# Holding the transposes of the attention queries in the middle of the next product's first piece

## The chip, the cores and the metric

The kernel runs on one core of one Trainium2 chip. The metric is the device time of one execution in microseconds (us); lower is better. The engines are named as in the profile: PE is TensorE's matmul, PEld its weight load, DVE VectorE, ACT ScalarE, POOL GpSimd, SP SyncE.

## What is computed

The program is a decoder trunk of two layers over 256 tokens of 2048 features, all in float32. Layer 0 mixes tokens with a state-space model, layer 1 with attention; each is followed by a SwiGLU feed-forward block of width 5632, with RMSNorm ahead of every block and at the end. The change lies in the attention of layer 1:

```python
qkv = x @ w_qkv + b_qkv                      # 2048 -> 2048 (32 query heads of 64) + 2 x 256 (4 key/value heads)
s = einsum(q, k) * HEAD_DIM ** -0.5          # blocks of 128 queries against a window of two blocks of keys
s = s - slopes * dist                        # ALiBi; then keys outside the window of 128 are masked
m = maximum(max(s), sink)
p = exp(s - m)
p = p / (sum(p) + exp(sink - m))
o = einsum(p, v)
return o @ w_o
```

## The kernel before

**Products.** Every big product is cut into pieces. A piece takes 512 rows by 512 columns of a weight matrix. Weights and activations are kept as two parts each, a rounded high part and the rest, and a product adds three matmuls (L922, L923, L924: high by high, high by low, low by high). With four slices `a` of 128 rows and two halves `t` of 128 tokens, a piece is 4 x 2 x 3 = 24 matmuls of 128x128 by 128x512. `linear` (L937) runs the four pieces of a product with 2048 rows and leaves two accumulators in PSUM, one for each `t`.

**Weights.** `W.next()` at the head of each piece keeps the split of the weights three pieces ahead and their loads five: SP issues the load into `raw` (L109), ACT writes the high part (L122), DVE the low part (L127).

**Order.** The program is traced once and a scheduler lays out each engine's instructions: where an instruction's inputs are not ready by its estimate, it places a later one that is. What is placed on an engine then runs in that order. `tc.keep_in_program_order(ins)` pins one instruction behind the one traced just before it on the same engine; it adds order and no wait. Work that belongs between pieces is put into lists of functions: `left`, drained by `linear` after each piece, and `slots`, of which `linear` and the loop over O's pieces take one entry after each piece.

**Attention.** The keys and values come first, then the queries in four chunks `c` of 512 columns (eight heads). For a chunk, `linear` makes the accumulators; ACT scales the bias (L1309, pinned), and DVE writes the queries `act` from the accumulator, the norm's factor and the bias, one instruction for each `t` (L1312). `heads(c, q)` makes the functions for the rest:

- `turn_q`: eight PE transposes of `act` into two PSUM tiles `tr` (L1224), copied into `qT` by DVE for `t` = 0 and by ACT for `t` = 1 (L1225);
- `scores(g4)`: for four heads the score products (L1237, L1238), then on DVE the ALiBi bias and mask (L1241), the maximum (L1243 to L1246) and `es` (L1248), on ACT the exponentials with their sums (L1253), on DVE the sums (L1255), their reciprocal (L1256) and the scaling (L1258); for c < 3 the probabilities are turned by DVE in blocks (L1267) and through DRAM by DMAs of POOL (L985, L986);
- `turned_s`: for c = 3 the probabilities are transposed by PE (L1281);
- `values(g4)`: the products with the values (L1292 to L1296), cast by ACT (L1299) and split by DVE (L1300) into `oT`.

The slots that follow chunk `c` stand between the pieces of the next product, that is chunk `c + 1` or, for c = 3, the first two column blocks of the output projection O. After the first piece come `turn_q` and `scores(0)`, after the second the values of the chunk before and `scores(1)`, and so on.

In the state-space layer, `piece` (L926) is also called with a function `late`: it is called in the middle of the piece, after two of the four slices, and the first matmul of each later product of the piece is pinned. In the attention layer it is called without one.

Of the kernel before, what the change touches and what calls it, by code (L numbers as in the profile page):

```python
# [17 lines left out]
P = 128  # L18
# [38 lines left out]
def kernel(  # L57
# [6 lines left out]
    V, S, PL, PE = nc.vector, nc.scalar, nc.gpsimd, nc.tensor  # L64
    uid = [0]

    def nm(s):
        uid[0] += 1
        return f"{s}_{uid[0]}"
# [10 lines left out]
    def bank(shape, name="ps"):  # L80
        return ps.tile(shape, F32, tag="ps", name=nm(name))


    def turned_tile(name):
        return pp.tile([P, 2, 4, T], F32R, tag="b8", name=nm(name))
# [96 lines left out]
    ident = cp.tile([P, P], F32, name="ident")  # L182
# [6 lines left out]
    left = []  # L189

    slots = []


    def s5(early_piece):
# [725 lines left out]
    def products(acc, xq, w, a, t, first, last, keep=lambda ins: ins):  # L920
        x_ = xq[:, :, a, t * P : (t + 1) * P]
        keep(PE.matmul(acc, x_[:, 0], w[0][:, a], start=first, stop=False))  # L922
        PE.matmul(acc, x_[:, 0], w[1][:, a], start=False, stop=False)  # L923
        PE.matmul(acc, x_[:, 1], w[0][:, a], start=False, stop=last)  # L924

    def piece(acc, xq, first, last, late=None):  # L926

        w = W.next()
        for a in range(4):
            keep = lambda ins: ins  # L930
            if a == 2 and late:
                late()
                keep = tc.keep_in_program_order
            for t in range(2):
                products(acc[t], xq, w, a, t, first and a == 0, last and a == 3, keep)

    def linear(xt, n_pieces=None, halves=False):  # L937


        n_pieces = n_pieces or len(xt)  # L940
        acc = [bank([P, 512], "acc") for _ in range(2)]
        if halves:
            ws = [W.next() for _ in range(n_pieces)]
            for t in range(2):
                for q in range(n_pieces):
                    for a in range(4):
                        products(acc[t], xt[q], ws[q], a, t, q == 0 and a == 0, q == n_pieces - 1 and a == 3)
            return acc
        for q in range(n_pieces):
            piece(acc, xt[q], q == 0, q == n_pieces - 1)  # L950
            n = -(-len(left) // max(1, n_pieces - 1 - q))
            for _ in range(n):
                left.pop(0)()
            if slots:
                for f in slots.pop(0):
                    f()
        return acc
# [129 lines left out]
    def glu(norm):  # L1087
        def load_h(c):
            for t in range(2):
                cs = slice(512 * c, 512 * c + 512)  # L1090
                tc.keep_in_program_order(nc.sync.dma_start(h[:, c, t], x[t * P : (t + 1) * P, cs]))

        for c in range(NCH):
            left.append(partial(load_h, c))
            if c == 0:
                pa, pb = accs
                for _, half, q in G_ORDER[EARLY:8]:
                    piece(accs[half], gt[q], q == 0, q == 3)
                    if left:
                        left.pop(0)()  # L1100
            else:
                pa = linear(gt)
                pb = linear(gt)
            act = wp.tile([P, 2, 512], F32, tag="act", name=nm("act"), bufs=2)
            for t in range(2):
                hc = h[:, c, t]
                sg = act[:, t]
                S.activation(sg, pb[t], AF.Sigmoid)
                V.tensor_tensor(sg, pa[t], sg, op=ALU.mult)
                V.tensor_tensor(hc, hc, sg, op=ALU.add)  # L1110
                norm.chunk(c, t)

    def swiglu(norm, out_norm):
# [14 lines left out]
        def gu(c):  # L1128
            last = c == FF_GROUPS[-1][-1]
            pg = linear(norm.xt)  # L1130
            if r[0] is None:
                r[0] = norm.scale()
            sg = wp.tile([P, 2, 512], F32, tag="act", name=nm("act"), bufs=2)
            for t in range(2):
                S.activation(sg[:, t], pg[t], AF.Silu, scale=r[0][:, t : t + 1])
            pu = linear(norm.xt)
            for t in range(2):
                V.scalar_tensor_tensor(sg[:, t], pu[t], r[0][:, t : t + 1], sg[:, t], ALU.mult, ALU.mult)
            if last:
                left.append(lambda: turned(c, sg))  # L1140
                return
            o, v = turned_tile("hT"), block_tile()
            ht[c] = o
            left.extend(partial(blocks_turned, v, sg, tb) for tb in range(4))

            def split():
                S.activation(o[:, 0], v, AF.Copy)  # L1147
                V.tensor_tensor(o[:, 1], v, o[:, 0].bitcast(F32), op=ALU.subtract)

            left.append(split)  # L1150
# [21 lines left out]
    def attention(norm, out_norm):  # L1172
        with tc.tile_pool(name="at", bufs=1) as ap:
# [15 lines left out]
            def bias(c):  # L1189
                b = ap.tile([P, 512], F32, tag="bias", name=nm("bias"))  # L1190
                nc.sync.dma_start(b, b_qkv[0, 512 * c : 512 * c + 512].unsqueeze(0).to_broadcast([P, 512]))
                return b
# [3 lines left out]
            acc = linear(norm.xt)  # L1196
# [17 lines left out]
            ot = []  # L1214

            def heads(c, q):
                st = {}

                def turn_q():
                    st["qT"] = ap.tile([P, 4, 2, P], F32, tag="qT", name=nm("qT"), bufs=2)  # L1220
                    for t in range(2):
                        pt = bank([P, 4, P], "tr")
                        for a in range(4):
                            PE.transpose(pt[:, a], q[:, t, a * P : (a + 1) * P], ident)  # L1224
                        (S.copy if t else V.tensor_copy)(st["qT"][:, :, t], pt)  # L1225
                    ot.append(turned_tile("oT"))

# [57 lines left out]
                def values(g4):  # L1285

                    v0, v1 = (kv[:, t, 256 + HD * c : 256 + HD * c + HD] for t in range(2))
                    for i2 in range(2):
# [11 lines left out]
                        V.tensor_tensor(ot[c][:, 1, a], v, ot[c][:, 0, a].bitcast(F32), op=ALU.subtract)  # L1300

                return turn_q, scores, turned_s, values

            late = []

            for c in range(4):
                b = bias(c)
                acc = linear(norm.xt)
                tc.keep_in_program_order(S.mul(b, b, HD ** -0.5))  # L1309
                q = wp.tile([P, 2, 512], F32, tag="act", name=nm("act"), bufs=2)  # L1310
                for t in range(2):
                    V.scalar_tensor_tensor(q[:, t], acc[t], r8[:, t : t + 1], b, ALU.mult, ALU.add)  # L1312
                turn_q, scores, turned_s, values = heads(c, q)
                turned = [partial(turned_s, g4) for g4 in range(2)] if c == 3 else []
                late = late or [lambda: None] * 2
                slots.append([turn_q, partial(scores, 0)])
                slots.append([late[0], partial(scores, 1)])
                slots.append(turned[:1])
                late, mine = [partial(values, 0), partial(values, 1)], late
                slots.append([mine[1], *late[: len(turned) // 2]])  # L1320
            slots.extend([turned[1:], late[1:]])

            accs = [[bank([P, 512], "acc") for _ in range(2)] for _ in range(2)]
            for n, q in O_ORDER[:8]:
                piece(accs[n], ot[q], q == 0, q == 3)
                if slots:
                    for f in slots.pop(0):
                        f()
            for n in range(NCH):
                acc = accs[n] if n < 2 else linear(ot, 4)  # L1330
# [6 lines left out]
    accs = []  # L1337
# [15 lines left out]
    swiglu(n0, n1)  # L1353
    n2 = Norm(2, (0, 1, 2))
    attention(n1, n2)
    swiglu(n2, Last(None))

# [27 lines left out]
```

## Time and profile before

| what | value |
|---|---|
| median of 3 runs | 1981.99 us (1981.92 to 1982.06) |
| profiled execution | 1981.87 us |
| its span, first to last instruction | 1980.0 us |
| granted TensorE clock, mean | 0.993 |
| eight transposes of L1224, by c | begin at 1064.45, 1091.25, 1122.82 and 1155.35 us |
| queries of L1312 | 8 instructions, median 744 ns |

A row of the time line has the start, the time in us, the engine, the line, the operation, out<-in with partitions x elements, and a count where like rows are merged; a bracket gives the engine's idle time ahead of the row and what ended it. Rows of waits have the waiting engine and line, what it waited for, the sum in us, the number of times and the longest. A row of stretches has the stretch, its length, the busy time and count of each engine (PE, PEld, DVE, ACT, POOL), the granted clock, the DMA share and GB/s. All times count from the span's start.

### The profile page before, as it was taken

To read this page: it belongs to the slowest core of one execution; us is meant where nothing else is said; L and a number is where in the kernel's file an instruction comes from. 1 tells how busy PE (TensorE), PEld (TensorE's weight loads), DVE (VectorE), ACT (ScalarE), POOL (GpSimd) and SP (SyncE) were. 2 spreads that over 40 slices of the span, in tenths; PEclk is the share of its full clock that TensorE was granted. 3 is DMA by queue.
4 is the path that set the end of the run, shared out by engine and by line. 5 is a ranking of instruction groups with operands and counts; after the bars stand their busy time and mean duration, and the time that the engine had idled before them with its cause. 6 is when DMAs were issued, how large, how long until landed. Compare 5 with 4: busy or idle time off the path is not lost.

```text
span 1980.0 us, 24858 instructions
## 1 busy us (share of the span) xinstructions
PE 1936.3 (98%) x10336; PEld 1601.1 (81%) x10336; DVE 1271.8 (64%) x1652; ACT 859.1 (43%) x839; POOL 127.5 (6%) x117
## 2 busy tenths in 40 slices
PE   7699999999999999999999999999999999999998
PEld 6578888888888888888888778888888888888886
DVE  8956665666556646665577888666654665466545
ACT  6554444343334333433455554533333433333333
POOL 6840000000000000000010110000000000000000
PEclk9899999999999999999999999999999999999999
DMA  4036665556565565656575864666566556655664
GB/s 131 24 106 220 213 212 185 187 186 208 191 191 192 191 200 182 207 188 201 179 266 177 264 217 152 201 197 196 192 191 191 191 191 196 197 190 189 206 191 149
DMA packets 187845, 373.20 MB, mean 188 GB/s; under 512 B 11122, under 2 KB 11186, under 8 KB 187604
## 3 DMA queue, kind: packets, MB, share of 16 engines
q1 hardware_dynamic: 183168, 356.87, 56.0%
q0 software_dynamic: 3728, 12.60, 1.9%
q10 hardware_dynamic: 836, 2.14, 0.3%
q8 instruction: 81, 1.33, 0.3%
q14 instruction: 32, 0.26, 0.0%
HBM read 363.19 MB, written 8.39 MB: 188 GB/s over the span
## 4 chain that ended last, share of the span: by engine, by line
PE 91%; DVE 6%; ACT 1%; issue 1%; DMA 1%; POOL 0%; DVEq 0%; ACTq 0%
PE acc L922 29%; PE acc L923 29%; PE acc L924 29%; DVE scan L573 1%; DVE w L127 1%; DVE V L578 1%; DVE V L576 1%; PE pv L210 1%; PE py L798 0%; DVE sc L1258 0%; DMA pd<-bt 0%; PE px L210 0%; DVE mx L1243 0%; DVE bt L1267 0%; DMA raw<-in_attn_w_qkv_dram 0%
## 5 line engine op out<-in xcount | busy, mean ns | idle before, releaser
L127 DVE TENSOR_TENSOR w<-raw,w 128x2048 fp32r<-128x2048 f32 x330 | 757.0, 2294 | 591.2 <-ACT w L122 589.1
L122 ACT ACTIVATE w<-raw 128x2048 fp32r<-128x2048 f32 x332 | 636.2, 1916 | 842.0 <-PE acc L924 561.7
L922 PE MATMUL acc<-w,xT 128*128 128x512 f32 x1568 | 611.3, 390 | 0.0
L924 PE MATMUL acc<-w,xT 128*128 128x512 f32 x1568 | 610.4, 389 | 0.0
L923 PE MATMUL acc<-w,xT 128*128 128x512 f32 x1568 | 610.1, 389 | 0.0
L922 PEld LDWEIGHTS acc<-w,xT 128*128 128x128 f32 x1568 | 294.4, 188 | 62.5 <-issue 1.8
L924 PEld LDWEIGHTS acc<-w,xT 128*128 128x128 f32 x1568 | 294.3, 188 | 61.6 <-issue 0.3
L923 PEld LDWEIGHTS acc<-w,xT 128*128 128x128 f32 x1568 | 294.4, 188 | 60.6
L922 PE MATMUL acc<-w,hT 128*128 128x512 f32 x704 | 274.3, 390 | 0.0
L923 PE MATMUL acc<-w,hT 128*128 128x512 f32 x704 | 273.6, 389 | 0.0
L924 PE MATMUL acc<-w,hT 128*128 128x512 f32 x704 | 273.3, 389 | 0.0
L922 PEld LDWEIGHTS acc<-w,hT 128*128 128x128 f32 x704 | 132.1, 188 | 28.5 <-ACT hT L1124 1.2
L924 PEld LDWEIGHTS acc<-w,hT 128*128 128x128 f32 x704 | 132.2, 188 | 27.5
L923 PEld LDWEIGHTS acc<-w,hT 128*128 128x128 f32 x704 | 132.2, 188 | 27.2
L994 DVE STREAM_TRANSPOSE bt<-act 32x256 f32<-32x256 f32 x320 | 139.6, 436 | 5.5
L923 PE MATMUL acc<-w,gt 128*128 128x512 f32 x256 | 99.7, 390 | 0.6 <-DVE w L127 0.6
L922 PE MATMUL acc<-w,gt 128*128 128x512 f32 x256 | 99.8, 391 | 0.0
L924 PE MATMUL acc<-w,gt 128*128 128x512 f32 x256 | 99.6, 389 | 0.0
L985 POOL DMA_DIRECT2D pd<-bt x36 | 19.7, 553 | 945.8 <-DVE bt L1032 842.8
L1147 ACT ACTIVATE hT<-bt 128x1024 fp32r<-128x1024 f32 x20 | 21.2, 1061 | 106.6 <-DVE bt L994 106.6
L1159 DVE TENSOR_TENSOR h<-h,acc 128x512 f32<-128x512 f32 x64 | 42.9, 685 | 22.0 <-PE acc L924 22.0
L923 PEld LDWEIGHTS acc<-w,gt 128*128 128x128 f32 x256 | 48.1, 188 | 10.8 <-DVE w L127 1.0
(253 smaller groups left out, 1275.5 us busy)
## 6 DMA issues: line engine op xcount, KB each, us to landing
raw<-in_ffn_w_gate_dram SPq DMA_DIRECT2D x88, 1024.0 KB, 5.2
raw<-in_ffn_w_up_dram SPq DMA_DIRECT2D x88, 1024.0 KB, 5.2
raw<-in_ffn_w_down_dram SPq DMA_DIRECT2D x88, 1024.0 KB, 5.1
raw<-in_s_w_glu_dram SPq DMA_DIRECT2D x32, 1024.0 KB, 5.3
raw<-in_attn_w_qkv_dram SPq DMA_DIRECT2D x20, 1024.0 KB, 5.3
raw<-in_attn_w_o_dram SPq DMA_DIRECT2D x16, 1024.0 KB, 5.2
pd<-bt POOLq DMA_DIRECT2D x24, 192.0 KB, 3.8
pT<-pd POOLq DMA_DIRECT2D x6, 768.0 KB, 5.9
```

What stands on the lines that cost most here:

```text
L122: keep(S.activation(w[:, 0], self.raw[i], AF.Copy))
L127: keep(e.tensor_tensor(lo, self.raw[i], hi.bitcast(F32), op=ALU.subtract))
L210: return (lambda *a, **k: pin(f(*a, **k))) if self.on else f
L573: keep(V.tensor_tensor(t_, ws[..., part], bc(Vt[hf][:, k - 1, :, part], 1, 2), op=ALU.mult))
L576: V.tensor_tensor(v, v, t_[:, 0], op=ALU.add)
L578: V.tensor_tensor(v, v, t_[:, 1, ::-1], op=ALU.add)
L922: keep(PE.matmul(acc, x_[:, 0], w[0][:, a], start=first, stop=False))
L923: PE.matmul(acc, x_[:, 0], w[1][:, a], start=False, stop=False)
L924: PE.matmul(acc, x_[:, 1], w[0][:, a], start=False, stop=last)
L994: V.transpose(dst[32 * q : 32 * q + 32, :, :, 32 * tb : 32 * tb + 32], src[:, :, :, 32 * q : 32 * q + 32])
L1147: S.activation(o[:, 0], v, AF.Copy)
L1159: V.tensor_tensor(hc, hc, acc[t], op=ALU.add)
```

## The change

`turn_q` leaves the slot after the first piece and goes to a list `mids`. The first piece of the next product takes it from there and calls it as `late`: after the slices a = 0 and 1, twelve matmuls, and ahead of a = 2 and 3. The first of the eight transposes is pinned behind the matmuls traced ahead of it. The first matmul (L922) of each of the four remaining products of that piece is pinned too, as `piece` does with any `late`. `scores(0)` stays in the slot after the piece.

```diff
+    mids = []
...
         for q in range(n_pieces):
-            piece(acc, xt[q], q == 0, q == n_pieces - 1)
+            piece(acc, xt[q], q == 0, q == n_pieces - 1, mids.pop(0) if mids else None)
...
                         for a in range(4):
-                            PE.transpose(pt[:, a], q[:, t, a * P : (a + 1) * P], ident)
+                            ins = PE.transpose(pt[:, a], q[:, t, a * P : (a + 1) * P], ident)
+                            if t + a == 0:
+                                tc.keep_in_program_order(ins)
...
-                slots.append([turn_q, partial(scores, 0)])
+                mids.append(turn_q)
+                slots.append([partial(scores, 0)])
...
             for n, q in O_ORDER[:8]:
-                piece(accs[n], ot[q], q == 0, q == 3)
+                piece(accs[n], ot[q], q == 0, q == 3, mids.pop(0) if mids else None)
```

## The prediction

> **What bounds the kernel now.** I read the page's busy times first, then busy time by stretches, then who waited for whom inside the attention stretch, then PE's instructions one by one there. The page:
>
> ```profile
> PE 1936.3 (98%) x10336; PEld 1601.1 (81%) x10336; DVE 1271.8 (64%) x1652; ACT 859.1 (43%) x839; POOL 127.5 (6%) x117
> ```
>
> TensorE (PE) is busy 98% of the span. By stretches (us, then busy us of PE, PEld, DVE, ACT, POOL, then clock and DMA):
>
> ```profile
> 1060.00:1200.00 140.00, 136.32 (x822) 108.92 (x821) 115.10 (x160) 75.74 (x183) 17.65 (x30) 1.00 0.66 215
> 1200.00:1980.00 780.00, 771.15 (x3409) 638.13 (x3407) 480.06 (x465) 314.77 (x230) 0.00 (x0) 1.00 0.59 190
> ```
>
> The change acts only between 1060 and 1200. Behind it PE is busy for 771 of 780 us, so nothing there gives back time that the attention stage loses or gains: what PE gains or loses here moves the end one for one. What PE waited for in 1060 to 1200 (us in total, times, longest):
>
> ```profile
> PE tr L1224 <- DVE act L1312: 2.0, 2, 1.3
> PE at L1237 <- DVE qT L1225: 1.0, 1, 1.0
> PE acc L922 <- DVE oT L1300: 0.3, 1, 0.3
> ```
>
> So two waits belong to the change: the transposes (L1224) wait for the queries `act` from L1312, and the score products (L1237) wait for the copies `qT` (L1225). The change moves the transposes. The question is whether their input is ready at the new place.
>
> **Where the transposes stand now.** A piece is 24 matmuls of L922 to L924. For c=2 PE does this (start, duration, line):
>
> ```profile
> 1115.34 0.50 PE L922 MATMUL acc<-w,xT 128*128 128x512 f32 x1
> ...
> 1121.14 0.39 PE L923 MATMUL acc<-w,xT 128*128 128x512 f32 x1
> 1122.82 0.66 PE L1224 MATMUL tr<-ident,act 128*128 128x128 f32 x4 [1.29 <-DVE act L1312]
> 1123.23 0.48 PE L924 MATMUL acc<-w,xT 128*128 128x512 f32 x1
> 1123.54 0.60 PE L1224 MATMUL tr<-ident,act 128*128 128x128 f32 x4
> ```
>
> The first matmul of the next product starts at 1115.34, the 26th at 1121.14: 5.80 / 25 = 0.23 us each, the price of a matmul below. The transposes stand behind 26 of them (a 27th between their halves), not behind 24 as the code has them, and even so PE waits. After the change they stand behind 12, at 1115.34 + 12 x 0.23 = 1118.1. Their input comes from DVE:
>
> ```profile
> 1119.34 0.17 DVE L1255 TENSOR_TENSOR sm<-sm,es 128x8 f32<-128x8 f32 x1 [3.59 <-ACT sc L1253]
> ...
> 1122.02 1.40 DVE L1312 SCALAR_TENSOR_TENSOR act<-acc,r,bias 128x512 f32<-128x512 f32 x2
> ```
>
> L1312 could not have gone into DVE's idle 3.59 us, because it reads the scaled bias of L1309, which the code pins on ACT behind what was traced ahead of it:
>
> ```profile
> 1115.59 0.40 ACT L1253 ACTIVATE sc<-sc,mx 128x128 f32<-128x128 f32 x1 [5.20 <-DVE mx L1246]
> ...
> 1119.73 0.63 ACT L1309 ACTIVATE bias<-bias 128x512 f32<-128x512 f32 x1
> ```
>
> The exponentials of the heads before run from 1115.59, L1309 ends at 1120.36. So `act` for c=2 hangs on DVE and ACT, not on PE, and a transposing PE that comes four microseconds earlier waits four microseconds longer.
>
> **The change part by part.** No instruction is added or removed: per c, eight transposes and two copies are issued in another place; no DMA is, and no queue of SP or POOL is passed. The pins are order alone, on PE: the first transpose behind the first 12 matmuls, the later L922s behind the transposes. Unlike now, the scheduler can no longer fill a wait for `act` with matmuls of the same product: the other 12 of the piece and the scores stand behind the waiting transposes, and ACT's weight casts (L122), which wait for PE to free a weight buffer, behind those. Each c by itself:
>
> c=0. The queries (DVE) and the transposes (PE) stand here:
>
> ```profile
> 1058.59 1.41 DVE L1312 SCALAR_TENSOR_TENSOR act<-acc,r,bias 128x512 f32<-128x512 f32 x2 [0.59 <-PE acc L924]
> ```
>
> ```profile
> 1064.45 1.03 PE L1224 MATMUL tr<-ident,act 128*128 128x128 f32 x8
> ```
>
> Twelve matmuls earlier is 1064.45 - 2.76 = 1061.7, and `act` is whole at 1060.0: no wait. Now the scores follow the copies too closely (waits of the weight load at PE, 1064 to 1074):
>
> ```profile
> PEld at L1238 <- ACT qT L1225: 0.4, 1, 0.4
> PEld at L1237 <- DVE qT L1225: 0.4, 1, 0.4
> ```
>
> After the change 12 matmuls, 2.8 us, cover the copies. The two waits bound the gain between 0 and 0.8; some of it overlaps matmuls that drain, so I take -0.4.
>
> c=1. `act` comes from the first row (DVE), and PE's transposes now start at the second:
>
> ```profile
> 1088.30 1.40 DVE L1312 SCALAR_TENSOR_TENSOR act<-acc,r,bias 128x512 f32<-128x512 f32 x2
> ```
>
> ```profile
> 1091.25 1.04 PE L1224 MATMUL tr<-ident,act 128*128 128x128 f32 x8
> ```
>
> The new place is 1091.25 - 2.8 - 0.4 = 1088.1. The halves of `act` are ready at about 1089.0 and 1089.7: PE waits about 0.95 for the first and, with 0.4 of transposes between, 0.25 for the second. +1.2; 0 if DVE moves forward with c=0.
>
> c=2. PE arrives at 1118.1 + 0.8 = 1118.9 and waits until 1122.8: 3.9 us. What counts is the state behind it: when the second half of the transposes ends, just before 1124, PE has now done 27 matmuls of the product, and after the change 12. It is 15 x 0.23 = 3.45 us behind, which already contains c=0 and c=1, as the wait swallows both. Bounds: 0 if `act` came 3.9 earlier, 3.9 + 1.2 if DVE shifts with the 1.2 of c=1. I keep 3.45, since the rows of DVE and ACT above name no PE work as the last releaser.
>
> c=3. The next product is that of O, PE's rows:
>
> ```profile
> 1146.38 0.50 PE L922 MATMUL acc<-w,oT 128*128 128x512 f32 x1
> ...
> 1154.26 0.39 PE L923 MATMUL acc<-w,oT 128*128 128x512 f32 x1
> 1155.35 0.63 PE L1224 MATMUL tr<-ident,act 128*128 128x128 f32 x4 [0.70 <-DVE act L1312]
> ...
> 1160.38 0.50 PE L1237 MATMUL at<-kT,qT 64*128 64x128 f32 x4 [0.98 <-DVE qT L1225]
> ...
> 1161.99 0.44 PE L1292 MATMUL po<-pT,kv 128*64 128x128 f32 x4
> ...
> 1163.45 0.48 PE L1237 MATMUL at<-kT,qT 64*128 64x128 f32 x2
> ...
> 1166.39 0.50 PE L922 MATMUL acc<-w,oT 128*128 128x512 f32 x1
> ```
>
> From 1146.38 to 1154.26 start 35 matmuls, and a 36th stands between the halves. PE arrives at 1146.38 + 3.45 + 2.8 = 1152.6; if `act` comes when it does now, it waits 2.7 until 1155.35, and is then 36 - 12 = 24 matmuls, 5.5 us, behind. From here it wins: the transposes, the first scores and the second now stand close together, and PE waits at each. It waits 0.98 for the copy; the second scores take 1166.39 - 1163.45 = 2.94 where the first take 1161.99 - 1160.38 = 1.61, so 1.33 is lost; and 0.34 goes in the wait for oT. With 12 matmuls behind the transposes and a whole piece between the scores these 2.65 should fill up. 5.5 - 2.65 = +2.85. Bounds: +5.5 where the same chain of copies keeps PE waiting; about -0.2 where `act` of c=3 comes as PE does (3.45 - 0.7 - 0.3 - 2.65).
>
> Sum: +2.85 on the profiled execution's 1981.87 (1980.0 of span and 1.87 around it), or 1984.7; the median, 0.12 above that execution, gives 1984.8. Forecast 1984.8, own range 1982 to 1987.5.
>
> **The rivals.** First, the clock falls as well. Early in this trace PE stood idle for 4.19 us, and its clock in the stretches that follow was half (the number behind POOL's):
>
> ```profile
> 20.91 1.94 PE L210 MATMUL pu<-ident,xs 128*128 128x128 f32 x8 [4.19 <-DVE xs L210]
> ...
> 20.00:24.00 4.00, 3.02 (x13) 2.68 (x14) 3.90 (x9) 1.69 (x3) 4.00 (x5) 0.50 0.00 0
> 24.00:28.00 4.00, 4.00 (x74) 3.37 (x73) 3.90 (x7) 2.36 (x5) 4.00 (x5) 0.81 0.02 4
> ```
>
> Half speed lasted from 20.91 to about 24 + 4 x 0.19 / 0.5 = 25.5, 4.6 us, and cost 2.3. The waits of now, 1.29 and 0.70, left the clock of 1060 to 1200 at 1.00. The wait of 3.9 at c=2 is nearer to 4.19 than to 1.29, so once is possible: 1984.8 + 2.3 = 1987.1, twice 1989.4. Against it: 3.9 is a little less, and shrinks if DVE moves forward. The Trainium skill, "TensorE: Matmul & The Clock Gate", section "What's actually happening", speaks against the change in the same way: an idle window of about 3.4 us halves the clock, and the window runs freely. By that rule a wait of 3.9 holds a whole window only at some phases, and the sum would be 1984.8 or 1987.1 by the phase; the 4.19 us row agrees with it.
>
> Second, faster: L1309 comes ahead of the exponentials. The scheduler lays out ACT anew, and only L1309's pin behind the casts of the values (L1299) is fixed, not its place against L1253. If L1309 (0.63) goes ahead of the exponentials that begin at 1115.59, it ends at 1116.2, or one or two steps of its size later if the casts L1299 go first; DVE is idle then, and `act` of c=2 is whole 1.4 later, at 1117.6 to 1118.5, ahead of PE's 1118.9: no wait is left. At c=2 alone that decides little; at c=3 also, all waits of now go: 0.4 + 1.3 + 0.7 + 2.65 = 5.05, so 1977 to 1979. It is decided by whether `act` comes 3.9 us sooner than now; what is less leaves a part of the wait. Against it: the exponentials are traced ahead of L1309 and were placed ahead of it at c=2 with ACT idle for 5.20 before.
>
> Third, no change: `act` of c=3 comes with PE, the -0.2 above, or the gains of c=0 and c=3 pay for c=2: 1981 to 1982.5.
>
> **How the numbers follow.** Forecast 0.50, clock 0.20, no change 0.20, faster 0.10. A difference of 0.2%, 4 us, is about what a measurement of this kernel can tell: the bounds are 1978.0 and 1986.0. Slower by more: the clock's 0.20 and the upper part of the forecast (over +4 of a top of +5.5), 0.14: 0.34. Faster by more: 0.07 of the 0.10. Within: 0.59. The range leaves out the faster half of the faster case and the twice fallen clock: 1980 to 1989.
>
> **What would show it.** In the changed kernel's trace the eight transposes of each c stand behind 12 matmuls and not 24 to 36; PE waits for `act` L1312 at c=1, 2 and 3, in sum 7 to 8 us in place of 2.0; "PE at <- DVE qT" is gone; the second scores of c=3 take 1.6 us. The prediction is wrong if ACT's or DVE's order around L1309 and L1312 has changed, so that `act` is there when PE comes, or if other matmuls fill the wait, or if the copies again hold up the scores.

## Result and the profile after

The changed kernel takes 1995.16 us (median of 5 runs, 1992.88 to 1995.93) against 1981.92 us before on the same chip: the ratio is 1.006, with a 95% interval of 1.0049 to 1.0071. It is slower by 13 us. The forecast was 1984.8 us with a range up to 1989: the sign was right and the size far too small. The profiled execution has a span of 1993.1 us against 1980.0.

The page's line of busy times, then two stretches of the changed kernel (us, then busy us of PE, PEld, DVE, ACT, POOL, then the granted clock):

```profile
PE 1941.4 (97%) x10336; PEld 1605.9 (81%) x10336; DVE 1273.1 (64%) x1652; ACT 858.6 (43%) x839; POOL 127.5 (6%) x117
```

```profile
1060.00:1200.00 140.00, 127.48 (x743) 101.62 (x743) 109.56 (x154) 70.67 (x177) 17.64 (x30) 0.95 0.63 201
1220.00:1993.00 773.00, 764.20 (x3378) 632.70 (x3377) 474.66 (x458) 311.52 (x225) 0.00 (x0) 1.00 0.59 191
```

PE is busy for 127.5 of the 140 us where it was busy for 136.3, and the clock of that stretch is no longer 1.00. What PE waited for there is now one row:

```profile
PE tr L1226 <- DVE act L1316: 12.5, 4, 6.3
```

(The lines have moved, those from L922 to L1224 by two and those from L1225 on by four: the transposes L1224 are L1226 now, the scaled bias L1309 is L1313, the queries L1312 are L1316, and the matmuls L922 to L924 are L924 to L926.) The waits for `qT` and for `oT` are gone, as forecast; the wait for the queries has grown from 2.0 to 12.5 us. PE at c=2:

```profile
1116.05 0.50 PE L924 MATMUL acc<-w,xT 128*128 128x512 f32 x1
...
1118.71 0.39 PE L926 MATMUL acc<-w,xT 128*128 128x512 f32 x1
1123.25 0.66 PE L1226 MATMUL tr<-ident,act 128*128 128x128 f32 x4 [4.15 <-DVE act L1316]
1125.57 1.12 PE L1226 MATMUL tr<-ident,act 128*128 128x128 f32 x4 [1.66 <-DVE act L1316]
1126.34 0.78 PE L924 MATMUL acc<-w,xT 128*128 128x512 f32 x1
...
1131.42 0.50 PE L1241 MATMUL at<-kT,qT 64*128 64x128 f32 x4
```

Twelve matmuls, then a wait of 4.15 us for the first half of the queries and 1.66 for the second, and then twelve matmuls that take 1131.42 - 1126.34 = 5.08 us up to the scores, 0.42 each on average and not 0.23. DVE in the same time:

```profile
1119.77 0.17 DVE L1259 TENSOR_TENSOR sm<-sm,es 128x8 f32<-128x8 f32 x1 [3.58 <-ACT sc L1257]
...
1122.45 0.74 DVE L1316 SCALAR_TENSOR_TENSOR act<-acc,r,bias 128x512 f32<-128x512 f32 x1
1123.11 1.77 DVE L1271 STREAM_TRANSPOSE bt<-sc 128x1536 f32<-128x1536 f32 x1
1124.80 0.71 DVE L1316 SCALAR_TENSOR_TENSOR act<-acc,r,bias 128x512 f32<-128x512 f32 x1
...
1132.38 1.02 DVE L1245 SCALAR_TENSOR_TENSOR sc<-nd,at 128x384 f32<-128x384 f32 x2 [4.07 <-PE at L1242]
...
1141.11 1.02 DVE L1245 SCALAR_TENSOR_TENSOR sc<-nd,at 128x384 f32<-128x384 f32 x2 [1.92 <-PE at L1242]
...
1162.80 1.37 DVE L1316 SCALAR_TENSOR_TENSOR act<-acc,r,bias 128x512 f32<-128x512 f32 x2
```

The first half comes as late as before (80.3 us behind PE's first transpose of the keys, in both), and a block transpose of 1.77 us now stands between the halves. Then DVE itself waits 4.07 us for PE's first scores and 1.92 for the second: the lateness has gone round. So at c=3 everything comes later, the queries (the last row above) and what follows on PE and on ACT:

```profile
1154.34 0.50 PE L924 MATMUL acc<-w,oT 128*128 128x512 f32 x1
...
1163.65 1.94 PE L1226 MATMUL tr<-ident,act 128*128 128x128 f32 x8 [6.30 <-DVE act L1316]
1165.24 0.78 PE L924 MATMUL acc<-w,oT 128*128 128x512 f32 x1
...
1169.70 0.50 PE L1241 MATMUL at<-kT,qT 64*128 64x128 f32 x4
```

```profile
1154.68 0.40 ACT L1257 ACTIVATE sc<-sc,mx 128x128 f32<-128x128 f32 x1 [5.16 <-DVE mx L1250]
...
1158.82 0.63 ACT L1313 ACTIVATE bias<-bias 128x512 f32<-128x512 f32 x1
```

In the kernel before, the exponentials ahead of the queries of c=3 (ACT) and these queries (DVE) stand here:

```profile
1148.14 0.39 ACT L1253 ACTIVATE sc<-sc,mx 128x128 f32<-128x128 f32 x1
```

```profile
1154.46 1.40 DVE L1312 SCALAR_TENSOR_TENSOR act<-acc,r,bias 128x512 f32<-128x512 f32 x2
```

PE waits 6.30 us for queries whose scaled bias (L1313) runs only behind the exponentials. The clock around both waits (the number behind POOL's):

```profile
1118.00:1122.00 4.00, 1.10 (x5) 0.56 (x3) 2.19 (x5) 4.00 (x12) 0.72 (x1) 1.00 1.02 359
1122.00:1126.00 4.00, 1.09 (x6) 0.85 (x7) 4.00 (x6) 0.60 (x1) 0.83 (x2) 0.77 0.10 40
1126.00:1130.00 4.00, 4.00 (x13) 3.24 (x12) 2.31 (x2) 0.59 (x1) 1.35 (x3) 0.50 0.93 258
...
1160.00:1164.00 4.00, 0.35 (x2) 0.38 (x3) 4.00 (x5) 1.25 (x1) 0.83 (x2) 0.71 0.35 138
1164.00:1168.00 4.00, 4.00 (x15) 3.42 (x14) 2.96 (x3) 0.59 (x1) 1.35 (x3) 0.50 0.78 198
```

Behind the 4.15 us the first four transposes of c=2 still take 0.66 us, as in the kernel before; behind the 1.66 us the next four take 1.12, and from there PE runs at half clock, as it does behind the 6.30 us of c=3.

**The bill.** What lies ahead of the attention stage differs by up to 2.3 us between profiled executions of equal code, so I compare the stage alone: from PE's first transpose of the keys (1041.77 before, 1042.14 after) to the first product of the last `values` (1194.72, 1207.77). It takes 152.96 us before and 165.63 after, +12.67. From there to the end it is 785.3 us in both: nothing was given back. By its parts:

- up to the product that follows the queries of c=2: +0.34 (-0.39 to the end of c=0's scores, then +0.73 at c=1);
- from there to the start of O: +7.25, of which waits of 4.15 + 1.66 for 1.29 before, and 2.2 for the twelve slow matmuls and 0.4 for slow transposes;
- from there to the last values: +5.08: a wait of 6.30 and 2.3 of half clock, less 3.35 of waits of before that are gone (0.70, 0.98, 1.33, 0.34); the parts add up to 5.25.

### The profile page after: what moved, and what is told of

It is laid out like the page before. It is cut to its first block, busy times and chain, and to the rows that moved or that the text cites. A ratio compares the mean times of both kernels' runs of the same rounds, so it can differ in the third digit from the quotient of the medians.

```text
span 1993.1 us, 24859 instructions
## 1 busy us (share of the span) xinstructions
PE 1941.4 (97%) x10336; PEld 1605.9 (81%) x10336; DVE 1273.1 (64%) x1652; ACT 858.6 (43%) x839; POOL 127.5 (6%) x117
## 3 DMA queue, kind: packets, MB, share of 16 engines
q8 instruction: 81, 1.33, 0.3%
## 4 chain that ended last, share of the span: by engine, by line
PE 91%; DVE 6%; ACT 1%; issue 1%; DMA 1%; POOL 0%; DVEq 0%; ACTq 0%
PE acc L924 29%; PE acc L925 29%; PE acc L926 29%; DVE scan L575 1%; DVE w L127 1%; DVE V L580 1%; DVE V L578 1%; PE pv L212 1%; DMA raw<-in_attn_w_qkv_dram 0%; DVE bt L1271 0%; PE py L800 0%; ACT sc L1257 0%; DVE sc L1262 0%; PE pm L756 0%; PE px L212 0%
## 5 line engine op out<-in xcount | busy, mean ns | idle before, releaser
L122 ACT ACTIVATE w<-raw 128x2048 fp32r<-128x2048 f32 x332 | 636.2, 1916 | 841.0 <-PE acc L926 532.5
L924 PE MATMUL acc<-w,xT 128*128 128x512 f32 x1568 | 613.2, 391 | 0.0
L926 PE MATMUL acc<-w,xT 128*128 128x512 f32 x1568 | 611.6, 390 | 0.0
L924 PEld LDWEIGHTS acc<-w,xT 128*128 128x128 f32 x1568 | 295.1, 188 | 62.8 <-issue 2.2
L926 PEld LDWEIGHTS acc<-w,xT 128*128 128x128 f32 x1568 | 295.1, 188 | 61.3
L924 PE MATMUL acc<-w,hT 128*128 128x512 f32 x704 | 274.6, 390 | 0.0
L926 PE MATMUL acc<-w,hT 128*128 128x512 f32 x704 | 273.7, 390 | 0.0
L924 PEld LDWEIGHTS acc<-w,hT 128*128 128x128 f32 x704 | 132.2, 188 | 28.3 <-ACT hT L1126 1.2
L926 PEld LDWEIGHTS acc<-w,hT 128*128 128x128 f32 x704 | 132.2, 188 | 27.4
L924 PE MATMUL acc<-w,gt 128*128 128x512 f32 x256 | 100.0, 391 | 0.0
L926 PE MATMUL acc<-w,gt 128*128 128x512 f32 x256 | 99.8, 390 | 0.0
```

Source lines behind the costliest of these rows:

```text
L122: keep(S.activation(w[:, 0], self.raw[i], AF.Copy))
```

## The experiments

Theory A: the cost is the distance to the queries, which come seven to nine us after the next product starts, because L1313 is pinned on ACT behind the exponentials of the heads before; each long wait costs half clock on top. Its rival B: the pins and the split piece cost by themselves, whenever the queries come. Times and stages of all kernels; each median stands beside the kernel before on the same chip; the stage is read from one profiled execution of each kernel, and only that of mid_nopin was taken twice:

| kernel | median us | before | ratio (95%) | stage us | to before's 152.96 |
|---|---|---|---|---|---|
| changed | 1995.16 | 1981.92 | 1.006 (1.0049 to 1.0071) | 165.63 | +12.67 |
| c01_mid | 1983.66 | 1982.13 | 1.0011 (1.0003 to 1.002) | 154.91 | +1.95 |
| c2_mid | 1990.17 | 1982.13 | 1.0042 (1.0029 to 1.0055) | 160.21 | +7.25 |
| c3_mid | 1986.73 | 1982.13 | 1.0025 (1.0015 to 1.0035) | 157.82 | +4.86 |
| mid_nopin | 1980.37 | 1982.13 | 0.9993 (0.9984 to 1.0002) | 150.01 | -2.95 |
| mid_nopin2 | 1980.67 | 1982.15 | 0.999 (0.9981 to 0.9999) | 150.00 | -2.96 |
| mid_nopin_c1 | 1979.69 | 1982.15 | 0.9985 (0.9976 to 0.9995) | 149.20 | -3.76 |
| slot_nopin | 1986.68 | 1983.05 | 1.002 (1.0011 to 1.0028) | 155.17 | +2.21 |
| mid_fill | 1990.83 | 1983.05 | 1.0041 (1.0028 to 1.0053) | 160.89 | +7.93 |
| mid_a3 | 1992.12 | 1983.05 | 1.0048 (1.0034 to 1.0062) | 162.61 | +9.65 |

**One chunk at a time.** c01_mid, c2_mid and c3_mid make the change for some chunks alone; shown is c2_mid:

```diff
-                            if t + a == 0:
+                            if t + a == 0 and c == 2:
...
-                mids.append(turn_q)
-                slots.append([partial(scores, 0)])
+                if c == 2:
+                    mids.append(turn_q)
+                slots.append(([] if c == 2 else [turn_q]) + [partial(scores, 0)])
```

> The new place for c=0 and c=1 alone; c=2 and c=3 as before. Theory A (the cost is a wait for the queries, which come a fixed seven to nine us after the next product starts at c=2 and 3, and the half clock after each long wait): almost nothing, 1981.5 to 1983, as the changed kernel's trace shows 0.7 us lost by the start of the product after c=2's queries. Theory B (the pins and the split piece cost by themselves, at every c alike): half of the 13 us, 1988.

> The new place for c=2 alone. Theory A: waits of 4 and 1 to 2 us and 2.2 us of half clock in place of 1.3, and the queries of c=3 move back by the same amount, as PE's delayed scores feed them: 1988 to 1989.5. The prediction's step (the queries of c=3 come at a fixed time, so a late PE waits less there): about 1985. Theory B: a quarter of 13, 1985.

> The new place for c=3 alone. Theory A: PE waits 6 us for the queries, then 2.3 us of half clock, and 3 to 4 us of waits of before go: 1986 to 1988; with c2_mid it adds up to the 13 us of the whole change. Theory B: a quarter of 13, 1985.

The stages add up to 1.95 + 7.25 + 4.86 = 14.06 for the whole change's 12.67, and are far from equal: B, which charges every c alike, is wrong. In detail A missed twice: both times came out above what it said. The stage of c01_mid was to lose nearly nothing and loses 1.95 us (the 0.7 us named in its expectation counts from the span's start; within the stage it is 0.34). The queries of c=3 came 1.9 us later in the stage there, although nothing was changed at c=3 and PE starts O 0.7 us earlier. PE's longest wait of its 4.0 us is there:

```profile
PE tr L1226 <- DVE act L1316: 4.0, 3, 3.3
```

The trace shows where that lateness starts. DVE, which had no such wait before, waits 3.94 us for a cast of the values (L1303), which stands on ACT behind a weight cast (L122), and that waits 4.45 us for its load:

```profile
1137.24 1.92 ACT L122 ACTIVATE w<-raw 128x2048 fp32r<-128x2048 f32 x1 [4.45 <-DMA raw<-in_attn_w_o_dram]
1139.06 0.35 ACT L1303 CAST oT<-po 128x256 fp32r<-128x256 f32 x1
```

```profile
1139.44 0.42 DVE L1304 TENSOR_TENSOR oT<-po,oT 128x256 fp32r<-128x256 f32 x1 [3.94 <-ACT oT L1303]
```

Why the load comes so late there was not followed. And in c2_mid, where PE starts O 5.7 us late within the stage, the first transposes of c=3 come 3.0 us late (116.56 us into the stage for 113.58), less than PE; PE then met another wait, for the probabilities of c=3, besides its 4.4 at c=2:

```profile
PE tr L1226 <- DVE act L1316: 4.4, 1, 4.4
PE tr L1285 <- DVE sc L1262: 3.1, 1, 3.1
```

In c3_mid, with no delay ahead of it, PE waits as long at c=3 as in the whole change, 5.9 us:

```profile
PE tr L1226 <- DVE act L1316: 6.6, 2, 5.9
```

**The queries made early.** mid_nopin is the whole change with one edit:

```diff
-                tc.keep_in_program_order(S.mul(b, b, HD ** -0.5))
+                S.mul(b, b, HD ** -0.5)
```

> The whole change, but the scaled bias (S.mul, L1313 of the changed kernel) is no longer pinned on ACT, so it can run as soon as the bias has landed. Theory A: the queries are there when PE comes, the waits for them (12.5 us in the changed kernel) fall under 2, the clock stays up, and the waits for the copies stay away too: 1977 to 1980, faster than the kernel before. Theory B: the place costs, not the queries: above 1990.

The stage falls by 15.62 us, from 165.63 to 150.01, with the transposes in the same place, the same pins and, on PE, the same order as in the changed kernel. DVE no longer makes the queries of c=2 behind the softmax but ahead of it:

```profile
1116.51 0.74 DVE L1316 SCALAR_TENSOR_TENSOR act<-acc,r,bias 128x512 f32<-128x512 f32 x1
...
1117.24 0.74 DVE L1316 SCALAR_TENSOR_TENSOR act<-acc,r,bias 128x512 f32<-128x512 f32 x1
```

and PE's transposes of c=2, which stand at 1119.75 there, wait for nothing. This is what PE still waits for:

```profile
PE acc L924 <- DVE sc L1245: 1.8, 1, 1.8
PE tr L1226 <- DVE act L1316: 0.4, 1, 0.4
```

That shows A against B: the place does not cost when its input is there. In the medians it is 1.8 us below the kernel before, where 1977 to 1980 had been expected, and the interval of the ratio still holds 1; the stage says -2.95.

**The control.** slot_nopin is the kernel before with that one edit and nothing else.

> The kernel before with one edit: the scaled bias is no longer pinned. The transposes stand in the slot after the first piece, as before. If the queries' lateness costs the kernel before its waits of 1.3 and 0.7 us: 1.5 to 3 us faster than before, stage of 150 to 151.5. Against mid_nopin (stage 150.0) it shows what the new place does with queries that are ready: 0 to 1 us better, if the cover for the copies is worth what the waits of 0.4 to 1.0 on qT say.

The expectation was wrong: it is slower than before, by 2.21 us in the stage and by 3.6 in the medians (the profiled execution was its fastest). No wait for the queries is left, but PE meets the copies (first row, PE), and ACT shows why (the other rows):

```profile
1127.84 0.48 PE L1242 MATMUL at<-kT,qT 64*128 64x256 f32 x1 [1.93 <-ACT qT L1229]
```

```profile
1124.89 0.63 ACT L1313 ACTIVATE bias<-bias 128x512 f32<-128x512 f32 x1 [2.76 <-DVE w L127]
1125.42 1.89 ACT L122 ACTIVATE w<-raw 128x2048 fp32r<-128x2048 f32 x1
1127.22 0.56 ACT L1229 COPY qT<-tr 128x512 f32<-128x512 f32 x1
```

The copy of t=1 stands behind the next chunk's bias and a weight cast. Where the scores follow the transposes at once, that is PE's wait; where twelve matmuls lie between, as in mid_nopin, it is not. Between these two kernels, whose queries are both ready, the new place is worth 155.17 - 150.01 = 5.16 us. PE's waits name 3.0 of it: 1.93 for the copies and 1.5 for probabilities that come through DRAM, less the 0.4 that mid_nopin waits at c=1. The rest was not taken apart. The change can gain, then; it had no input to work on.

**The clock by itself.** mid_fill keeps PE at work while it waits. In `turn_q`, ahead of the transposes of the first half:

```diff
+FILL = (0, 0, 16, 25)
...
+                        for k in range(FILL[c] if t == 0 else 0):
+                            xq, w = here
+                            ins = PE.matmul(pt.rearrange("p a b -> p (a b)"), xq[:, 0, k % 2, 0:P], w[0][:, k % 2], start=True, stop=True)
+                            tc.keep_in_program_order(ins)
```

> The whole change, and ahead of the transposes of c=2 and c=3 stand 16 and 25 more matmuls (3.7 and 5.8 us) whose result is thrown away, so that PE works while it waits and its clock stays up. They fit into the waits of the changed kernel (4.1 and 6.3 us). If the half clock behind the waits is a part of the loss by itself: 4.5 us faster than the changed kernel, about 1990.5 or a stage (from the keys' transposes to the last product with the values) of 161 in place of 165.6. If the clock only looks low because PE is idle: no faster than the changed kernel, 1995.

More work, less time: the stage is 160.89, 4.74 us below the changed kernel. PE still waits 0.33 and 0.47 us for the queries behind the filling, so the added matmuls hold up no transpose. The stretches behind the two waits run at full clock:

```profile
1124.00:1128.00 4.00, 2.34 (x15) 1.84 (x14) 4.00 (x3) 0.59 (x1) 2.19 (x4) 1.00 0.30 67
1162.00:1166.00 4.00, 3.90 (x24) 3.00 (x24) 2.93 (x3) 0.86 (x2) 1.32 (x3) 1.00 0.81 204
```

So of the 12.67 us some 4.7 are half clock and 7.9 the waits, net of those that went. The Trainium skill, "TensorE: Matmul & The Clock Gate", section "What's actually happening", says that the clock falls after an idle window; the run agrees.

**Six matmuls later.** mid_a3 holds the transposes behind 18 of the 24 matmuls:

```diff
-            if a == 2 and late:
+            if a == at and late:        # 3 for the attention's pieces
```

> The whole change, but held six matmuls (1.4 us) later, behind 18 of the 24. Theory A (distance to the queries): the waits at c=2 and 3 shorten by 1.4 us each, the wait at c=2 falls to about 2.8 us, under that which halves the clock, so 3 to 5 us faster than the changed kernel, 1990 to 1992, stage of 160.5 to 163. Theory B (pins and split piece): no change, 1995.

1992.12 us and a stage of 162.61, 3.02 us below the changed kernel, as A has it. But the reason was partly another: the wait at c=2 did shorten, to 3.02 us, and the clock fell all the same (at c=3 PE waits 3.49 and 1.20 us, and it falls there too):

```profile
1124.26 1.97 PE L1226 MATMUL tr<-ident,act 128*128 128x128 f32 x8 [3.02 <-DVE act L1316]
```

```profile
1124.00:1128.00 4.00, 3.74 (x15) 3.37 (x16) 4.00 (x4) 0.59 (x1) 1.16 (x3) 0.60 0.32 72
```

**A version that beats both.** mid_nopin_c1 is mid_nopin with c=1 alone held behind 18 matmuls; mid_nopin2 is mid_nopin again.

```diff
-                mids.append(turn_q)
+                mids.append((turn_q, 3 if c == 1 else 2))
```

> The new place with the unpinned bias, and c=1 held six matmuls later than the others (behind 18 of the 24), since mid_nopin still waited 0.7 us for the queries there and the change behind 18 waited for none. If distance to the queries is all: stage 0.5 to 0.8 us below mid_nopin's 150.0, so 149.3, and 1978 to 1980, 2 to 3.5 us faster than before. If the copies of c=1 are then no longer covered: no gain over mid_nopin or a loss.

> mid_nopin once more, on another draw: stage of 150.0 again, 2 to 3 us less than before in the medians (1978.5 to 1980.5 beside 1982). If the stage comes out above 152, its gain was chance.

The stage of mid_nopin came out equal to 0.01 us. mid_nopin_c1 gains another 0.80 there and is the fastest kernel: 1979.69 for 1982.15, 0.9985 (0.9976 to 0.9995), or 0.15% less time. Its only wait of PE in the stage is the 1.8 us for L1245.

## Why the prediction was wrong

- **The wait and its cause: right.** PE arrives at c=2 behind twelve matmuls, at 1118.9 as worked out, and waits for the queries (now L1316), which stand behind ACT's pinned bias. mid_nopin shows the cause. In sum PE waits 12.5 us for them where 7 to 8 was put.
- **c=0 and c=1: right.** -0.4 was put for c=0, and the stage shows -0.39 there; at c=1 +1.2 was put and +0.73 measured, with a wait of 0.41.
- **c=2: mis-sized.** The term was a lag of 3.45 us behind the kernel before; when O starts, PE is 0.34 + 7.25 = 7.59 us behind. Two things were left out. The halves of the queries were taken to follow each other as in the profile of before, but the scheduler laid DVE out anew and put a transpose between them (1.66 us of wait). And the half clock (2.6). Without these two the lag is 3.33, near the term.
- **c=3: the step that failed.** I had the queries of c=3 come at the time of before, so that a late PE would wait only 2.7 us. They come 120.66 us into the stage for 112.69, 7.97 later, about as late as PE, and PE waits 6.30. They hang on the scores of c=2, and these on PE: on the way to them DVE waits 4.07 + 1.92 us for PE's scores, where in the kernel before it waited for none. That this is all of the 7.97 is not shown: c01_mid has them 1.9 late with PE early, and c2_mid 3.1 late with PE 5.7 late. A wait that feeds the chain which it waits for is not swallowed by it. What was to come back at c=3 did come back: 2.65 was put, and those waits are gone. As the wait at c=3 decides when PE goes on, the prediction's sum can be done again with it: 2.85 + 7.97 + 2.3 of half clock behind this wait is 13.1, for 12.67 measured. (The lower bound of c=3 takes off 0.3 that no row beside it names; the forecast does not use it.)
- **The clock: the rival with a chance of 0.20 came in, twice.** Its price, 2.3 each, was right (2.6 and 2.3, and 4.74 for both in mid_fill). The forecast plus two of them was 1989.4; most of the rest is the split queries of c=2 and the late ones of c=3.
- **The faster rival** named the right switch, L1309 against the exponentials, but the scheduler did not turn it by itself; turned by hand it gives 150.01, not the 147.9 that 5.05 us less would be.

## What to carry to other kernels

Before a step is moved ahead in an engine's queue, find out when its input is made, and follow that back through every engine to what is pinned: here an operation of 0.6 us, pinned on ACT, held up TensorE. If the chain behind the input starts from the waiting engine itself, a delay goes round and is paid at each turn, so do not take the input's time from the old profile as fixed. Price an idle time of TensorE of some 3 us or more with the half clock that can follow it.

## What was not expected of the hardware

The clock does not follow the length of a wait alone. In mid_a3 it fell at a wait of 3.02 us; in c01_mid PE waited 3.31 us and the clock stayed up:

```profile
1158.71 0.63 PE L1226 MATMUL tr<-ident,act 128*128 128x128 f32 x4 [3.31 <-DVE act L1316]
```

```profile
1158.00:1162.00 4.00, 3.29 (x19) 2.86 (x20) 4.00 (x4) 0.59 (x1) 0.76 (x1) 1.00 0.73 242
```

How soon it falls differs too. In mid_a3 (first row) the mean of 0.76 puts the fall at 1123.76, 2.5 us after PE's last matmul ended by the profile (2.9 after its start). In the changed kernel at c=2 (second row) it comes at 1124.15, 5.0 us after the matmul that ended at 1119.10, with four transposes in between. In the wait of 4.19 us of the kernel before, which the prediction reads, it falls at 18.70, 2.0 us into the wait (third row):

```profile
1123.50:1124.00 0.50, 0.00 (x0) 0.00 (x0) 0.50 (x2) 0.10 (x1) 0.00 (x0) 0.76 0.02 6
```

```profile
1124.00:1124.50 0.50, 0.00 (x0) 0.00 (x0) 0.50 (x1) 0.00 (x0) 0.00 (x0) 0.65 0.00 0
```

```profile
18.50:19.00 0.50, 0.00 (x0) 0.00 (x0) 0.43 (x3) 0.00 (x0) 0.50 (x2) 0.70 1.01 381
```

A window of measurement that runs freely, as the page of the Trainium skill named above has it, would give such a difference by the phase; but its window of about 3.4 us is longer than the time in which the clock fell in mid_a3 and in the 4.19 us row, which the prediction took to agree with it. No run here fixes the phase.
